# First value products ahead of the scores and of the last block's store, the next S5 unit's tables behind the key product, and one S5 scale from sums of squares

## The chip, the cores and the metric

One core of a Trainium2 chip runs the whole program: one layer of a sequence encoder for one sequence of 2048 positions. The metric is the device time of one launch in microseconds, as the median of several runs. A core has five engines, each with a queue of instructions that it takes strictly in order: TensorE (PE, matrix products and transposes), VectorE (DVE), ScalarE (ACT), GpSimd (POOL) and SyncE (SP, which here only issues DMAs). They wait for each other through semaphores.

## The reference, cut to what matters

```
h = rmsnorm(x, norm_mix_g);  p = h @ w_in
u, q_raw, k_raw, v, o_raw, i_raw, f_raw = split(p)      # 512 | 4x512 | 4 | 4
# S5: 32 groups of 16 channels, a diagonal complex state of 64 per group
x_t = a * x_{t-1} + B u_t;   y = Re(C x) + d * u
z = gelu(y);  z = z * sigmoid(z @ w_glu + b_glu);  y_ssm = rmsnorm(z)
# mLSTM: 4 heads of 128, gated matrix memory
q, k = silu(causal_conv4(q_raw, k_raw))
h = (decayed scores q k^T) v + q C_state, over its normaliser;  y_ml = rmsnorm(sigmoid(o) * h)
x = x + concat(y_ssm, y_ml) @ w_out
x = x + relu(rmsnorm(x) @ w_ff1)^2 @ w_ff2;  return rmsnorm(x)
```

## The kernel before

Every product that matters is made of float16 pairs: each operand is split into a high and a low half, and `mm3` issues three matmuls for each step over the 128 rows of the contraction (lines 168 to 170). So the weights are scaled by a power of two per matrix before they are split (`load_w`), and the S5 output `z` is scaled the same way before the GLU product.

The program has four stages. The start normalises x, transposes it into `xn`, and makes the S5 inputs and the gates. Then comes the mixer, which the change touches: one loop over 16 blocks `b`, block b being head b // 4 and quarter b % 4 of the positions (512 of them). Behind it stand the rest of the GLU with the output projection, and the feed-forward network, two thirds of the time, which the change leaves alone.

A turn of the mixer's loop issues, in the order of the text: `proj_qk(b+1, 0)`, the query product of the next block; `mix_store(b-1)`, which transposes the last block's output (`pT`, line 931), splits it (`mo`) and sends it to memory; `mix_scores(b)`, which makes the decay tables `sc` and `dm`, transposes the keys (`pK`, line 864) and multiplies keys by queries (`pS`, line 867); `proj_vo(b, 0)` and `proj_vo(b, 1)`, the value and output-gate products (`pv`), 48 matmuls each; between and behind them the S5 units; `mix_state(b)`; `proj_qk(b+1, 1)`, the key product; and `mix_out(b)`. `mix_out` ends with a chain that the store of the next turn needs: `og` on DVE (line 913), squares on ACT (915), a few 128x4 steps on DVE (918 to 920), a power on POOL (921), one more step on DVE (922), and the scaling of `og` on ACT (924). The transposes `pT` read that `og`. Behind the key or query product stand the convolution on DVE (three steps of line 256) and SiLU (lines 258 and 259).

The S5 part is cut into 16 units u of two groups. `s5_const(u)` makes the unit's tables: `inm` and `xt`, the small products `pgg` and `pit`, and the rotation table `rh` on POOL and DVE, which four DMAs on SP's queue copy into `rt` (line 696). `s5_state(u)` transposes the inputs (`put`), multiplies them (`pw`), rotates by `rt` on DVE and POOL (lines 722 to 724), scans (726), and rotates back into `sv`. `s5_out(u)` multiplies out (`py`, lines 744 and 745), makes the GELU (748 to 752: ACT squares, DVE, ACT tanh, DVE) and writes `uz`. After every fourth unit two reductions over 128x1024 elements (line 756) take the largest magnitude of `uz`, one for each half of the positions, into `zmx`; `glu_open` in block 11 makes a power of two for each half from it (lines 775 to 783).

The order in which the instructions stand on each engine is not that of the text. When the program is built, a list scheduler goes through it with durations of its own, takes for each engine the earliest instruction of the text that it believes to be ready, and fixes the queues. The text is its priority. So a changed order of calls moves instructions only as far as the scheduler follows, and the order it fixed does not change at run time. PSUM tiles are taken in turn from small pools: three banks tagged `ml` (`pT`, `pK`, `pS`, `pst`, `pn`, and the GLU's `pz` and `pgT`), three tagged `mm` (the large products), two tagged `ax` (the S5 products).

## Time and profile before

| | us |
|---|---|
| median of 3 runs (lowest to highest) | 2136.23 (2135.05 to 2136.75) |
| the profiled execution's own time | 2138.6 |
| its span, first to last instruction | 2136.9 |
| DVE busy in the stretch 140 to 563 us (most of the mixer) | 337.34 |
| ACT busy there | 236.25 |
| POOL busy there | 199.39 |

The profile is one execution. Its time is 2.4 us above the median, and 1.7 us of it lie outside the span. A row of the timeline gives the start, the duration, the engine, the line, and in brackets how long the engine had been idle before it and what ended that. Line numbers are those of the kernel before. Matmuls are pipelined: what a matmul costs is the distance to the next start, not its duration. Tile names in the rows of the order carry their block or unit: `pT5` is the store of block 5, `og11` the output of head 1, quarter 1, which is block 5, `pv120` the first value product of head 1, quarter 2, which is block 6.

### The profile page before, as it was taken

Reading aid. Unit: us, or ns where it says so; the run is one execution under the profiler, and the core shown is the slowest. Engines: PE = TensorE matmul, PEld = TensorE weight load, DVE = VectorE, ACT = ScalarE, POOL = GpSimd, SP = SyncE. Lnnn points to the kernel's source line nnn. Section 1 sums busy time; section 2 is a strip of 40 time slices with the busy share of each in tenths; the row PEclk is TensorE's granted clock in tenths of the full one; section 3 lists DMA queues with packets and bytes.
Section 4 is the critical chain, followed back from the end, with each engine's and each line's share of the span. In section 5 each row is a group of like instructions: output and inputs, shape, how many; then the busy total and the mean of one; then the engine's idle time right before and its main releaser. Section 6 shows DMA issues by size and latency. Waiting matters only on the chain.

```text
span 2136.9 us, 29966 instructions
## 1 busy us (share of the span) xinstructions
PE 2032.5 (95%) x11237; PEld 1157.3 (54%) x11237; DVE 1676.3 (78%) x2743; ACT 1080.7 (51%) x2027; POOL 1072.1 (50%) x976
## 2 busy tenths in 40 slices
PE   6999898998999999999999999999999999999997
PEld 4897676766667454444444444444444444444445
DVE  7887878886857776767888989987878787777775
ACT  4435556564545423365545545455655545555543
POOL 1014546453211102586766675585776666565644
PEclk9999999999999999999999999999999999999998
DMA  5111211111203242312122132124433322121012
GB/s 188 62 53 50 61 40 48 62 45 55 80 21 109 99 197 93 110 60 79 64 90 83 60 99 79 65 90 181 148 129 104 109 104 79 43 77 59 21 40 79
DMA packets 57027, 177.10 MB, mean 83 GB/s; under 512 B 8048, under 2 KB 21552, under 8 KB 43312
## 3 DMA queue, kind: packets, MB, share of 16 engines
q1 hardware_dynamic: 56880, 175.17, 24.5%
q8 instruction: 88, 1.44, 0.3%
q14 instruction: 59, 0.48, 0.1%
HBM read 138.35 MB, written 28.41 MB: 78 GB/s over the span
## 4 chain that ended last, share of the span: by engine, by line
PE 58%; DVE 22%; POOL 7%; issue 4%; DMA 4%; ACT 3%; SPq 1%; POOLq 0%; DVEq 0%; ACTq 0%
PE fx L1421 4%; PE fx L1422 4%; PE fx L1423 3%; PE gx L1421 3%; PE gx L1423 3%; PE gx L1422 3%; PE po L168 3%; PE po L169 3%; PE po L170 3%; DVE w2o L1288 3%; DVE y L256 2%; PE fv L1423 2%; PE fv L1422 2%; PE fv L1421 2%; DVE x L1517 2%
## 5 line engine op out<-in xcount | busy, mean ns | idle before, releaser
L1422 PEld LDWEIGHTS <-w2o 128*128 128x128 f16 x952 | 93.4, 98 | 123.8 <-issue 27.6
L1450 ACT ACTIVATE e<-e 128x512 f32<-128x512 f32 x96 | 60.3, 628 | 193.2 <-DVE e L1486 92.5
L1423 PEld LDWEIGHTS <-w2o 128*128 128x128 f16 x952 | 93.4, 98 | 105.0 <-DVE w2o L1288 3.6
L1421 PEld LDWEIGHTS <-w2o 128*128 128x128 f16 x952 | 93.7, 98 | 104.0 <-issue 2.7
L169 PE MATMUL pv<-w_vo,xn 128*128 128x256 f16 x512 | 142.2, 278 | 1.5 <-DVE w_vo L153 1.5
L168 PE MATMUL pv<-w_vo,xn 128*128 128x256 f16 x512 | 142.5, 278 | 0.8 <-ACT w_vo L152 0.7
L170 PE MATMUL pv<-w_vo,xn 128*128 128x256 f16 x512 | 142.4, 278 | 0.0
L1287 ACT ACTIVATE w2o<-r,fs_b 128x512 f16<-128x512 f32 (+1 forms) x96 | 78.9, 823 | 109.5 <-POOL r L1345 50.1
L1288 DVE SCALAR_TENSOR_TENSOR w2o<-r,fs_b,w2o 128x512 f16<-128x512 f32 (+1 forms) x96 | 104.5, 1091 | 25.7 <-ACT w2o L1287 25.4
L1517 DVE SCALAR_TENSOR_TENSOR x2b<-gx,dd,x2b 128x512 f32<-128x512 f32 x112 | 82.9, 745 | 43.4 <-PE gx L1423 43.1
L1345 POOL TENSOR_TENSOR r<-r,s 128x256 f32<-128x256 f32 x64 | 64.8, 1013 | 104.1 <-DVE w2o L1288 104.1
L1517 DVE SCALAR_TENSOR_TENSOR x<-gx,dd,x 128x512 f32<-128x512 f32 x128 | 94.4, 742 | 10.6 <-PE gx L1423 10.3
L168 PE MATMUL pq<-xn,w_qk 128*128 128x512 f16 x256 | 97.9, 383 | 0.0
L169 PE MATMUL pq<-xn,w_qk 128*128 128x512 f16 x256 | 97.5, 381 | 0.0
L1421 PE MATMUL fx<-hop,wB 128*128 128x512 f16 x256 | 97.1, 379 | 0.4 <-ACT e L1479 0.4
L170 PE MATMUL pq<-xn,w_qk 128*128 128x512 f16 x256 | 97.3, 380 | 0.0
L1422 PE MATMUL fx<-hop,wB 128*128 128x512 f16 x256 | 97.1, 379 | 0.0
L1423 PE MATMUL fx<-hop,wB 128*128 128x512 f16 x256 | 97.1, 379 | 0.0
L168 PEld LDWEIGHTS <-xn 128*128 128x128 f16 x768 | 88.3, 115 | 12.8 <-ACT xn L457 3.3
L170 PEld LDWEIGHTS <-xn 128*128 128x128 f16 x768 | 88.1, 115 | 10.6 <-issue 2.1
L169 PEld LDWEIGHTS <-xn 128*128 128x128 f16 x768 | 88.4, 115 | 9.2
L1301 POOL TENSOR_TENSOR s<-r 128x512 f32<-128x512 f32 x32 | 52.8, 1650 | 76.6 <-issue 65.8
(1378 smaller groups left out, 6911.0 us busy)
## 6 DMA issues: line engine op xcount, KB each, us to landing
r<-in_w_dram SPq DMA_DIRECT2D x64, 1024.0 KB, 4.9
xt<-in_xN_dram SPq DMA_DIRECT2D x16, 512.0 KB, 3.7
rt<-rh SPq DMA_DIRECT2D x64, 128.0 KB, 2.3
hopd<-ho SPq DMA_DIRECT2D x28, 256.0 KB, 2.6
hop<-hopd SPq DMA_DIRECT2D x7, 1024.0 KB, 4.9
st_vo<-in_wvo_dram SPq DMA_DIRECT2D x4, 1024.0 KB, 5.1
bcm<-negM_d SPq DMA_DIRECT2D x16, 256.0 KB, 3.2
ml_d<-mo SPq DMA_DIRECT2D x16, 256.0 KB, 2.4
```

The costliest lines, as they stand in the source:

```text
L168: T.matmul(out, wh, xh, start=(i == 0), stop=False)
L169: T.matmul(out, wh, xl, start=False, stop=False)
L170: T.matmul(out, wl, xh, start=False, stop=(i == n - 1))
L1287: S.activation(out=hi, in_=src, func=AF.Copy, scale=sg)
L1288: V.scalar_tensor_tensor(out=lo, in0=src, scalar=sg, in1=hi, op0=ALU.mult, op1=ALU.subtract)
L1301: G.tensor_tensor(out=s12[:, 0], in0=raw[:, 2], in1=raw[:, 3], op=ALU.add)
L1345: G.tensor_tensor(out=r[:, 1], in0=r[:, 1], in1=s12[:, 1], op=ALU.subtract)
L1421: T.matmul(out, wh, xh, start=(first and i == 0), stop=False, skip_group_check=True)
L1422: T.matmul(out, wh, xl, start=False, stop=False, skip_group_check=True)
L1423: T.matmul(out, wl, xh, start=False, stop=(last and i == n - 1), skip_group_check=True)
L1450: S.activation(out=x, in_=x if src is None else src, func=AF.Relu, scale=scale)
L1517: V.scalar_tensor_tensor(out=acc[:, j, c, :], in0=bk[b], scalar=dd, in1=acc[:, j, c, :], op0=ALU.mult, op1=ALU.add)
```

## The change

It has three parts. First, in each turn `proj_vo(b, 0)` and `mix_scores(b)` are issued ahead of `mix_store(b-1)`; in block 11 `proj_vo(11, 0)` so also stands ahead of the last S5 output and of `glu_open`. The last store, `mix_store(15)` behind the loop, stays where it was. Second, the tables of the next S5 unit are still issued right behind a unit's state where another unit of the same block follows, but behind the key product `proj_qk(b+1, 1)` where the unit is the block's last: that is ten of the fifteen units made inside the loop (2, 3, 5, 6, 8, 9, 11, 12, 14, 15). Third, the eight reductions of line 756 are gone; the ACT square of each unit also gives its sum over the free elements (`accum_out`), and `glu_open` makes one scale for both halves from the sixteen sums, by halving the exponent of their total.

```diff
+    def sq_pow2(ss, mp):
+        V.tensor_scalar(out=ss, in0=ss, scalar1=1e-30, scalar2=None, op0=ALU.max)
+        V.tensor_scalar(out=mp.bitcast(I32), in0=ss.bitcast(I32), scalar1=1, scalar2=None, op0=ALU.logical_shift_right)
+        V.tensor_scalar(out=mp.bitcast(I32), in0=mp.bitcast(I32), scalar1=0x7F800000, scalar2=None, op0=ALU.bitwise_and)
+        V.tensor_scalar(out=mp, in0=mp, scalar1=2.0 ** 64, scalar2=None, op0=ALU.mult)
...
-    zmx = gcon.tile([P, 2, 4], F32, name="zmx")
+    zss = gcon.tile([P, 16], F32, name="zss")
...
-        S.activation(out=y2, in_=py, func=AF.Square)
+        S.activation(out=y2, in_=py, func=AF.Square, accum_out=zss[:, u:u + 1])
...
-        if u % 4 == 3:
-            m = u // 4
-            for h in range(2):
-                V.tensor_reduce(out=zmx[:, h, m:m + 1], in_=uz[h][:, 8 * m:8 * m + 8, :].rearrange("p g n -> p (g n)"), axis=AX.X, op=ALU.max, apply_absolute_value=True)
...
-        zm, zi, zs, zd, zo = (gp.tile([P, 2], F32, name=f"z{n}") for n in "misdo")
-        V.tensor_reduce(out=zm, in_=zmx, axis=AX.X, op=ALU.max)
-        V.tensor_scalar(out=zm, in0=zm, scalar1=1e-6, scalar2=None, op0=ALU.max)
-        V.tensor_scalar(out=zi.bitcast(I32), in0=zm.bitcast(I32), scalar1=0x7F800000, scalar2=None, op0=ALU.bitwise_and)
+        zm, zi, zs, zd, zo = (gp.tile([P, 1], F32, name=f"z{n}") for n in "misdo")
+        V.tensor_reduce(out=zm, in_=zss, axis=AX.X, op=ALU.add)
+        sq_pow2(zm, zi)
...
         if b >= 1:
+            proj_vo(b, 0)
+        mix_scores(b)
+        if b >= 1:
             mix_store(b - 1)
-        mix_scores(b)
         if b == S5_BLOCKS:
...
-        if b >= 1:
-            proj_vo(b, 0)
...
             s5_state(u)
-            if u + 1 < 16:
+            if u + 1 < 16 and i + 1 < len(us_):
                 s5_const(u + 1)
...
         if 1 <= bn < 16:
             proj_qk(bn, 1)
+        if us_ and us_[-1] + 1 < 16:
+            s5_const(us_[-1] + 1)
```

How the queues moved is shown at three places. The first is block 10, on PE. Before, 33 of the 48 matmuls of `pv220` stand ahead of the store's transposes `pT9`, which are mixed with the key transposes and the scores, and the other 15 stand behind:

```order
L170 MATMUL pv220_6011<-w_vo2_4708,xn1_105 128x256
L931 MATMUL pT9_5970<-ident_72,og21_5634 128x128
L864 MATMUL pK10_5995<-ident_72,y221_5861 128x128 x2
...
L867 MATMUL pS10_5996<-y220_5582,y221_5861 128x128 x3
L168 LDWEIGHTS xn1_105
L168 MATMUL pv220_6011<-w_vo2_4708,xn1_105 128x256
```

After, on PE at the same place, all 48 matmuls, the key transposes and the scores stand ahead of `pT9`, and the S5 output `py14` comes right behind it:

```order
L177 MATMUL pv220_5967<-w_vo2_4704,xn1_105 128x256
L867 MATMUL pK10_6034<-ident_72,y221_5813 128x128 x4
L870 MATMUL pS10_6035<-y220_5576,y221_5813 128x128 x4
L934 MATMUL pT9_6047<-ident_72,og21_5590 128x128 x4
L751 MATMUL py14_6056<-m00_144,us14_5752 128x128
```

On ACT at that place, the scaling of `og21` (what `pT9` waits for) stood right behind the two halves of a weight split, and ahead of the evacuation of the key product `pq230`; before:

```order
L152 ACTIVATE w_qk3_5909<-st_qk3_5907,sg_qk3_5922 128x1024 x2
L924 ACTIVATE og21_5634<-og21_5634,v49_5897 128x128 x4
L245 ACTIVATE xc230_5960<-pq230_5934 128x512
L246 ACTIVATE y230_5959<-pq230_5934,cb2_4307,cw2_4305 128x512
L248 COPY xc231_6195<-hl221_5866 128x3
```

After, on ACT, that evacuation is ahead of it:

```order
L159 ACTIVATE w_qk3_5903<-st_qk3_5901,sg_qk3_5916 128x1024 x2
L252 ACTIVATE xc230_5954<-pq230_5928 128x512
L253 ACTIVATE y230_5953<-pq230_5928,cb2_4303,cw2_4301 128x512
L255 COPY xc231_6189<-hl221_5818 128x3
L927 ACTIVATE og21_5590<-og21_5590,v49_5891 128x128 x4
```

So `pT9` comes 15 matmuls, the key transposes and the scores later on PE, and `og21` three instructions later on ACT. In the other blocks the same table of rows, cut down to what stands ahead of `pT`, reads: in blocks 2 and 4, six matmuls of `pv` and `pK` and `pS` more than before; in blocks 3 and 7, `pK` and `pS` more and three matmuls less; in blocks 5 and 9, 23 matmuls and `pK` and `pS` more.

The second place is block 6, where the scheduler did otherwise. On PE before, the S5 output `py8` (eight rows, the last two shown) and two matmuls of the second value product stand ahead of `pT5`:

```order
L744 MATMUL py8_4437<-m00_144,us8_4133 128x128
L745 MATMUL py8_4437<-xt8_3809,sv8_4152 128x128
L168 LDWEIGHTS xn1_105
L168 MATMUL pv121_4452<-w_vo1_3083,xn1_105 128x256
L169 LDWEIGHTS xn1_105
L169 MATMUL pv121_4452<-w_vo1_3083,xn1_105 128x256
L931 MATMUL pT5_4345<-ident_72,og11_4007 128x128
L864 MATMUL pK6_4370<-ident_72,y121_4236 128x128 x2
```

After, on PE, `pK6` and `pS6` stand ahead of it and `py8` behind:

```order
L177 MATMUL pv120_4344<-w_vo1_3081,xn1_105 128x256
L867 MATMUL pK6_4411<-ident_72,y121_4190 128x128 x4
L870 MATMUL pS6_4412<-y120_3953,y121_4190 128x128 x4
L934 MATMUL pT5_4424<-ident_72,og11_3967 128x128 x4
L751 MATMUL py8_4433<-m00_144,us8_4129 128x128
```

On DVE, the small steps `v45` that lead to `og11` were mixed with the two halves of a weight split and a convolution step; before:

```order
L919 TENSOR_TENSOR v45_4272<-v45_4272,rc5_4250 128x4
L153 SCALAR_TENSOR_TENSOR w_qk2_4284<-st_qk2_4282,sg_qk2_4297,w_qk2_4284 128x1024
L920 TENSOR_SCALAR v45_4272<-v45_4272 128x4
L153 SCALAR_TENSOR_TENSOR w_qk2_4284<-st_qk2_4282,sg_qk2_4297,w_qk2_4284 128x1024
L256 SCALAR_TENSOR_TENSOR y130_4334<-xc130_4335,cw1_2051,y130_4334 128x512
L922 SCALAR_TENSOR_TENSOR v45_4272<-v45_4272,rc5_4250 128x4
```

After, on DVE, the step ahead of POOL's power comes first, and one half of the split lies between it and the last step:

```order
L922 TENSOR_TENSOR v45_4268<-v45_4268,rc5_4246 128x4
L923 TENSOR_SCALAR v45_4268<-v45_4268 128x4
L160 SCALAR_TENSOR_TENSOR w_qk2_4280<-st_qk2_4278,sg_qk2_4293,w_qk2_4280 128x1024
L925 SCALAR_TENSOR_TENSOR v45_4268<-v45_4268,rc5_4246 128x4
L160 SCALAR_TENSOR_TENSOR w_qk2_4280<-st_qk2_4278,sg_qk2_4293,w_qk2_4280 128x1024
```

So PE has not more but less work ahead of `pT5`, and DVE's steps for it come one half of a split sooner. The third place is ACT behind the loop, where the last store (whose call did not move) waits for `og33`; before:

```order
L811 ACTIVATE gth8_7993,vg8_7997<-zc8_7835 128x512
L144 ACTIVATE w_out2_8003<-st_o2_6416,sg_out2_8018 128x256 x8
L924 ACTIVATE og33_7775<-og33_7775,v415_7953 128x128 x4
L808 ACTIVATE gth9_8119<-gth9_8119 128x512
L827 ACTIVATE ms0_6361<-pgT7_8089 128x8x64
```

After, on ACT:

```order
L798 ACTIVATE zt9_7971<-pz9_7966 128x512
L151 ACTIVATE w_out2_7997<-st_o2_6464,sg_out2_8012 128x256 x4
L927 ACTIVATE og33_7733<-og33_7733,v415_7947 128x128 x4
L151 ACTIVATE w_out2_7997<-st_o2_6464,sg_out2_8012 128x256 x4
L811 ACTIVATE gth9_8113<-gth9_8113 128x512
```

Four of the eight pieces of the weight split moved behind `og33`. SP's queue keeps its order but for one pair: the store of block 10 now stands ahead of two loads in block 11 instead of behind them. On POOL the instructions of `rh` keep the order among themselves; of their neighbours one has changed sides with them, or with a step between them, in units 4, 7, 8, 10 and 15.

More of the change, by code (lines that the diff above doesn't have):

```diff
@@ L787, in glu_a @@
         gp = gl["p"]
-        zs = gl["z"][1][:, h:h + 1]
+        zs = gl["z"][1]
         zc = gp.tile([P, 512], F32, name=f"zc{n}", tag="zc", bufs=3)
@@ L801, in glu_b @@
         gp = gl["p"]
-        zi, _, zd, zo = (a[:, h:h + 1] for a in gl["z"])
+        zi, _, zd, zo = gl["z"]
         zc, zt = gl[n]
```

## The prediction

> **What bounds the kernel now.** I read the page first, then stretches of the span, then the waits of the mixer, then the chain of waits.
>
> ```profile
> span 2136.9 us, 29966 instructions
> 140.00:563.00 423.00, 390.21 (x2817) 303.24 (x2816) 337.34 (x663) 236.25 (x639) 199.39 (x207) 0.98 0.20 56
> 712.00:2000.00 1288.00, 1268.96 (x5907) 584.03 (x5906) 1024.73 (x1314) 643.57 (x957) 774.07 (x638) 1.00 0.27 92
> PE pT L931 <- ACT og L924: 20.3, 10, 3.9
> PE pgg L662 <- DVE t L722: 6.4, 4, 2.7
> ```
>
> In the two stretches the numbers behind the length are busy times of PE, weight loads, DVE, ACT and POOL, then the granted clock. In the feed-forward network PE is busy for 1268.96 of 1288 us, and nothing of the change is there. In the mixer it is busy for 390.21 of 423 us: 33 us are to be had. The last two rows are PE's waits of that stretch: ten times it waited at the store's transposes `pT` until ACT had scaled `og`, 20.3 us in all. That is what the first part of the change is about. These are the waits on which my sum rests, and two behind them (566.16 is the GLU's first product, 704.61 the last store):
>
> ```profile
> 227.49 0.33 PE L931 MATMUL pT<-ident,og 128*128 128x128 f32 x1 [1.61 <-ACT og L924]
> 263.81 0.62 PE L931 MATMUL pT<-ident,og 128*128 128x128 f32 x2 [2.34 <-ACT og L924]
> 373.72 0.33 PE L931 MATMUL pT<-ident,og 128*128 128x128 f32 x1 [3.91 <-ACT og L924]
> 514.96 0.47 PE L931 MATMUL pT<-ident,og 128*128 128x128 f32 x1 [3.25 <-ACT og L924]
> 566.16 0.61 PE L168 MATMUL pgl<-w_glu,zt 128*128 128x512 f16 x1 [2.13 <-ACT zt L795]
> 704.61 0.33 PE L931 MATMUL pT<-ident,og 128*128 128x128 f32 x1 [2.20 <-ACT og L924]
> ```
>
> Not every wait of PE is worth its length. The chain of waits runs through PE behind each of these six, but through the other ten-odd waits of the mixer it does not: there it runs on DVE, POOL and the copies of the rotation tables, and PE only follows. So I count a wait fully only where the chain passes it. Its share by line between 425 and 520 us shows how little PE it holds:
>
> ```profile
> by line: DVE y L256 13.6%; DMA rt<-rh 11.6%; issue 10.8%; SPq L696 7.5%; DVE t L726 6.1%; POOL rh L629 3.9%; POOL t L629 3.3%; DVE t L724 2.7%; POOL v L921 2.6%; DVE rh L632 2.4%; DVE t L722 2.1%; ACT w_qk L152 2.1%; DVE uz L752 2.1%; POOL
> ```
>
> **A wait costs more than its length.** Behind such a wait PE runs at half clock:
>
> ```profile
> 265.10:268.50 3.40, 3.40 (x19) 3.09 (x18) 3.40 (x6) 3.06 (x7) 1.33 (x2) 0.51 0.41 171
> 374.40:377.80 3.40, 3.40 (x18) 3.03 (x18) 3.07 (x5) 2.47 (x6) 1.06 (x3) 0.50 0.52 219
> 514.90:517.70 2.80, 2.74 (x13) 2.74 (x14) 2.42 (x3) 2.54 (x8) 0.00 (x0) 0.50 0.31 72
> 566.10:568.90 2.80, 2.74 (x7) 1.05 (x8) 2.77 (x5) 0.00 (x1) 0.00 (x0) 0.50 0.72 208
> 705.40:708.80 3.40, 3.17 (x14) 2.26 (x13) 3.32 (x10) 2.65 (x7) 0.00 (x0) 0.51 0.00 0
> ```
>
> The clock is the third number from the right. Each stretch is about 3.4 us long, so it holds 1.7 us of work less than at full clock. They follow waits of 2.34, 3.91, 3.25, 2.13 and 2.20 us; behind the 1.61 us at 227.49 there is none. A wait that shrinks below about 2 us should therefore also save 1.7 us.
>
> [...]
>
> **Part 1, the new order.** What is put ahead of `pT` is priced by the distance between starts:
>
> ```profile
> 196.32 0.38 PE L864 MATMUL pK<-ident,y 128*128 128x128 f32 x2
> 196.54 1.06 PE L867 MATMUL pS<-y,y 128*128 128x128 f32 x8
> 197.43 0.27 PE L169 MATMUL pv<-w_vo,xn 128*128 128x256 f16 x1
> 197.54 0.27 PE L170 MATMUL pv<-w_vo,xn 128*128 128x256 f16 x1
> 367.65 0.39 PE L744 MATMUL py<-m,us 128*128 128x128 f32 x2
> 369.44 0.27 PE L168 MATMUL pv<-w_vo,xn 128*128 128x256 f16 x1
> ```
>
> Two `pK` take 0.22 us, so four take 0.44; a block's scores take 0.89; a `pv` matmul 0.11; a whole `py` 369.44 - 367.65 = 1.79. `pK` and `pS` together are 1.33.
>
> Block 2: six `pv` and 1.33 make 1.99 us of work in a wait of 1.61: all of it goes, 1.6. Block 3: 1.33 less three `pv` is 1.0 of 2.34; 1.3 us remain, too short for the half clock: 1.0 + 1.7 = 2.7. Block 10: fifteen `pv` (1.65) and 1.33 make 3.0. But `og21` now stands behind three more instructions on ACT:
>
> ```profile
> 514.52 1.26 ACT L924 ACTIVATE og<-og,v 128x128 f32<-128x128 f32 x4
> 515.81 0.60 ACT L245 ACTIVATE xc<-pq 128x512 f32<-128x512 f32 x1
> 516.97 0.19 ACT L248 COPY xc<-hl 128x3 f32<-128x3 f32 x1
> ```
>
> From 515.81 to the end of the last one are 1.35 us by which `og21` comes later. The wait becomes 3.25 + 1.35 - 3.0 = 1.6; 1.65 + 1.7 = 3.3.
>
> Block 6 is the exception. `pT5` has 1.33 more ahead of it but loses `py8` and two `pv` (1.79 + 0.22), so PE comes to it 0.7 us sooner, and only an earlier `og11` helps. The chain that leads there:
>
> ```profile
> 354.89 1.13 DVE zmx L756
> 356.62 1.13 DVE zmx L756
> 369.63 1.20 DVE w_qk L153
> 370.83 0.09 DVE v L920
> 370.99 2.00 POOL v L921
> ```
>
> Two of the removed reductions lie on it (2.26 us; they are part 3, but paid here), and the half of the weight split ahead of line 920 (1.2) now stands behind it, beside POOL's power. That is 3.46 of the 3.91 us, and the slow stretch: 5.2. `py8` follows the wait instead of filling the time ahead of it, which costs nothing as long as the wait is gone.
>
> The last store: four pieces of the weight split no longer stand ahead of `og33`.
>
> ```profile
> 700.97 3.30 ACT L144 ACTIVATE w_out<-st_o,sg_out 128x256 f16<-128x256 f32 x8 [1.12 <-DVE sg_out L125]
> ```
>
> Half of 3.30 is 1.65 of the 2.20 us; with the slow stretch 3.3.
>
> The store's own work, its two splits and its DMA, only shifts. Nothing reads what it stores before the loop's end, and on SP it passes two loads in block 11 alone. Its bank of PSUM is next taken by `pn`, which stands a whole key product later, so nobody waits for it. In block 6 `pK6` may wait a moment for its key (line 259 on DVE); that step lies on the chain of `og11` and comes sooner with it, so it adds nothing behind.
>
> **Part 2, the tables.** Their work stays the same, DMAs included. It is moved past the key product on PE, past its convolution on DVE, and, on SP and POOL, past nothing: there the rows of `rh` keep their order. I cost it at nothing. What hides it is the time between the tables and the next unit's rotation. The trace shows no case with them later, so bounds: a gain of 6.4 us, if PE's waits at `pgg` (quoted above) all go, and a loss, worked out below as a rival. I take zero, since the order hardly follows the text here.
>
> **Part 3, the scale.** Eight reductions leave DVE. Two are counted in block 6, two stand between the GLU's weight load and its product:
>
> ```profile
> 555.39 0.68 DVE L869 TENSOR_TENSOR kw<-pK,gcol 128x512 f32<-128x512 f32 x1
> 556.65 2.34 DVE L756 TENSOR_REDUCE zmx<-uz 128x1 f32<-128x1024 f32 x2
> L915 ACT ACTIVATION_READ_ACCUMULATOR kw<-og x64: 185/187/218, 182.4 to 698.2; 128x1 f32 x64
> ```
>
> There 2.3 us go. `kw` moves ahead into the wait for the load, while a step of the same size (`y215`) comes in its place. Two more steps on 128x1 elements come in. The product waited 2.13 us; that wait goes, and its slow stretch: 2.1 + 1.7 = 3.8. The other four reductions are off the chain. Against it, sixteen sums are read out on ACT, 0.19 us each as in the last row (a square with the same read-out elsewhere), 3.0 us; ACT is on the chain only here and there, so I charge a third, 1.0.
>
> **The sum.** 1.6 + 2.7 + 3.3 + 5.2 + 3.3 + 3.8 - 1.0 = 18.9 us. I don't take all of it. Behind each wait the chain goes back to DVE and POOL for some 10 to 80 us, and there the queues were dealt out anew as well, in places for the worse (`og21` above). I take two thirds, 12.6, a choice and not a row. The profiled execution took 2138.6 us, so it would take 2126.0; the median of the runs is 2.4 below it. So the forecast is 2123.7 us.
>
> **The rivals.**
>
> *The waits go and come back elsewhere.* PE comes sooner to places that DVE, POOL or a table's copy sets, as in the shares above. Then only the two pairs of reductions and little else count, within 4 us: about 2134. For it speaks how little PE the chain holds from 425 to 520 us; against it that the six waits I count are those which the chain passes.
>
> *All waits at `pT` go, on the chain or not.* The ten waits, each cut by what the order puts ahead of it in blocks 1 to 10: 0.6, 1.6, 1.0, 2.0, 1.1, 3.5, 1.0, 1.0, 1.1, 1.6, which is 14.5 of the 20.3; 2.1 and 1.7 behind them; six slow stretches (a sixth follows the wait of block 4), 10.2; less 1.0. That is 27.5: 2138.6 - 27.5 - 2.4 = 2108.7. Against it: PE isn't on the chain there.
>
> *Only DVE's part acts*, the scheduler having kept PE's order where it mattered, as in block 6: 3.5 and 2.1 and no slow stretch, 5.6 less 1.0: 2131.6. The shown rows of block 10 speak against it.
>
> *The slow stretches stay.* They might hang on the pattern of work around, not on the wait alone. [...] The five rows speak against it. [...]
>
> *Slower: the tables come late.* The scheduler may let the three convolution steps go ahead of DVE's half of `rh`, and a late copy stops the rotation at once. The rows are the first and the last of the eight copies on the chain, a convolution step, and a rotation that waited:
>
> ```profile
> 195.20 2.32 DMA rt<-rh
> ...
> 496.66 2.36 DMA rt<-rh
> 372.01 0.75 DVE L256 SCALAR_TENSOR_TENSOR y<-xc,cw,y 128x512 f32<-128x512 f32 x1
> 481.62 0.69 DVE L722 TENSOR_TENSOR t<-pw,rt 128x512 f32<-128x512 f32 x1 [1.25 <-DMA rt<-rh]
> ```
>
> Three steps are 2.25 us for a unit, 22.5 for the ten that moved. The chain passes eight of fifteen copies, so 12.0 of it would show. PE would lose its gain to these waits, and only DVE's part (4.6 as above) would stay: 12.0 - 4.6 is 7.4 more than the median of 2136.2, 2143.6. The sign turns when four of the ten units come late (4 x 2.25 x 8/15 = 4.8). The last row shows that there is no slack; the kept order of `rh` on POOL speaks against it.
>
> **How the numbers follow.** The chances: forecast 0.47; waits come back 0.16; all go 0.12; slow stretches stay 0.10; only DVE's part 0.06; slower 0.09. The range takes in all but the last, with some room: 2108 to 2138. About 0.2% (4.3 us) is what a measurement of this kernel can tell from no change: faster 0.75, same 0.16, slower 0.09.
>
> **What would show it.** Right: the waits that stood at 263, 373, 514 and 704 us are below 2 us, no half clock stands behind them, PE's waits on `og` from 140 to 563 us sum to less than 8 us, and the GLU's first product doesn't wait. Wrong: the same idle time of PE in the mixer under other names, `pgg`, `py` or `put`; rows of line 722 waiting for `rt` by 2 us or more; or a wait at `pT5` as long as before, since there the order gives PE nothing to do.

## The result and the profile after

The changed kernel takes 2120.91 us (median of 4 runs, 2116.55 to 2122.24), the kernel before 2135.64 us (4 runs, 2131.21 to 2136.75): a ratio of 0.9926, with a 95% interval of 0.9911 to 0.9941. The forecast was 2123.7 us. Measured once more on another chip (`e9_again`, below), the gain was 13.9 us instead of 14.7.

The page, the stretches and the waits of PE in the mixer, for the changed kernel, in the columns that the prediction used. Line numbers are now those of the changed kernel: `pT` is line 934, the scaling of `og` 927, `pgg` 669, the rotation's first step 729.

```profile
span 2118.6 us, 29982 instructions
```

```profile
140.00:553.00 413.00, 386.93 (x2801) 299.65 (x2798) 331.85 (x657) 239.04 (x660) 199.26 (x207) 0.99 0.20 57
712.00:2000.00 1288.00, 1269.47 (x5919) 584.40 (x5918) 1025.79 (x1311) 645.82 (x956) 778.45 (x640) 1.00 0.27 92
```

```profile
PE pgg L669 <- DVE t L729: 9.9, 5, 3.2
PE pT L934 <- ACT og L927: 6.7, 6, 1.5
PE py L752 <- POOL sv L741: 3.3, 6, 0.9
PE pgg L669 <- DVE uz L759: 2.4, 2, 1.2
```

The same piece of the mixer is 10 us shorter. The waits at `pT` fell from 20.3 to 6.7 us, those at `pgg` grew from 7.0 (6.4 + 0.6) to 12.3, and those at `py` from 2.1 to 4.3. PE's idle time as a whole fell only from 32.8 us (423.00 - 390.21) to 26.1 (413.00 - 386.93): half of what went at `pT` came back elsewhere. The rows of the timeline at the places of the prediction (blocks 3, 6, 10 and the last store), and two waits that are new or longer, at `pgg3` and at `pst`:

```profile
261.95 0.33 PE L934 MATMUL pT<-ident,og 128*128 128x128 f32 x1 [1.34 <-ACT og L927]
367.81 0.33 PE L934 MATMUL pT<-ident,og 128*128 128x128 f32 x1 [1.32 <-ACT og L927]
507.69 0.62 PE L934 MATMUL pT<-ident,og 128*128 128x128 f32 x2
687.96 0.33 PE L934 MATMUL pT<-ident,og 128*128 128x128 f32 x1 [0.81 <-ACT og L927]
219.88 0.40 PE L669 MATMUL pgg<-xt,ge 128*128 128x16 f32 x2 [3.17 <-DVE t L729]
555.36 0.80 PE L889 MATMUL pst<-vt,kw 128*128 128x129 f32 x2 [2.28 <-DVE C L894]
```

Between the first scores and the feed-forward network PE ran at half clock in eight windows of 3.4 us before and in three after. The third of these stands at the opening of the GLU, where one stood before (at 565.5 us); the other two are new. The clock is the third number from the right:

```profile
220.40:223.90 3.50, 3.50 (x19) 2.81 (x19) 3.46 (x9) 1.31 (x3) 1.29 (x1) 0.51 0.02 5
476.40:479.90 3.50, 3.50 (x19) 2.52 (x18) 3.46 (x7) 0.87 (x2) 1.66 (x2) 0.51 0.00 0
555.00:558.40 3.40, 3.04 (x8) 1.41 (x9) 3.17 (x8) 0.00 (x0) 0.00 (x0) 0.51 0.65 205
```

Where the time went can be read from the first matmul of some tiles on PE in the two timelines (us from the start of the span). Each line's gain is the step of the shift from the line above it; beside it the term of the prediction's sum, before the two thirds. The last column tells how many matmuls more (or less) than before PE runs between the two marks: where it isn't 0, the new order has moved matmuls across a mark, and gain or loss is in part only that.

| PE's first matmul of | before | after | shift | gained | term | matmuls |
|---|---|---|---|---|---|---|
| `pS0`, the first scores | 164.73 | 161.89 | -2.84 | | not of the change | |
| `pw2`, in block 1 | 211.46 | 209.30 | -2.16 | -0.7 | | 0 |
| `pw3`, block 2 | 242.20 | 240.34 | -1.86 | -0.3 | 1.6 | 0 |
| `pw5`, block 3 | 283.94 | 279.50 | -4.44 | 2.6 | 2.7 | -10 |
| `pw8`, blocks 4 and 5 | 348.67 | 346.93 | -1.74 | -2.7 | | +13 |
| `pw9`, block 6 | 387.46 | 381.08 | -6.38 | 4.6 | 5.2 | -3 |
| `pw14`, blocks 7 to 9 | 494.47 | 488.03 | -6.44 | 0.1 | | +3 |
| `pw15`, block 10 | 531.96 | 520.96 | -11.00 | 4.6 | 3.3 | -3 |
| `pgl3`, the GLU's opening | 599.52 | 588.93 | -10.59 | -0.4 | 3.8 | 0 |
| `po0`, with the last store | 706.49 | 691.43 | -15.05 | 4.5 | 3.3 | +4 |
| `fx`, feed-forward network | 902.75 | 886.79 | -15.96 | 0.9 | | -4 |
| end of the span | 2136.86 | 2118.64 | -18.22 | 2.3 | not of the change | |

So only sums of lines with equal work can be held against the terms. Idle is the time in which PE ran no matmul:

| stretch | gained | terms | idle before, after | windows at half clock |
|---|---|---|---|---|
| block 1 | -0.7 | | 2.1, 2.8 | 0, 0 |
| block 2 | -0.3 | 1.6 | 4.3, 3.2 | 0, 1 |
| blocks 3 to 6 | 4.5 | 7.9 | 11.3, 10.4 | 3, 0 |
| blocks 7 to 10 | 4.6 | 3.3 | 13.4, 8.1 | 1, 1 |
| the GLU's opening | -0.4 | 3.8 | 3.9, 3.9 | 1, 1 |
| last store, up to `fx` | 5.4 | 3.3 | 7.9, 6.7 | 3, 0 |

From the first scores to the network, where the change acts, 13.1 us are gained. The 2.8 and 2.3 us outside are the spread of single executions: the profiles of `e2_tables` and `e3_scale`, below, which gain nothing, are 3.9 and 1.6 us earlier than that of before at the first scores too.

### The profile page after: what moved, and what is told of

It reads as the page before. It is cut to its first block, busy times and chain, and to the rows that moved or that the text cites. A ratio compares the mean times of both kernels' runs of the same rounds, so it can differ in the third digit from the quotient of the medians.

```text
span 2118.6 us, 29982 instructions
## 1 busy us (share of the span) xinstructions
PE 2024.7 (96%) x11237; PEld 1152.8 (54%) x11237; DVE 1670.2 (79%) x2737; ACT 1080.5 (51%) x2043; POOL 1074.6 (51%) x976
## 4 chain that ended last, share of the span: by engine, by line
PE 56%; DVE 25%; DMA 6%; POOL 6%; issue 4%; ACT 3%; SPq 1%; POOLq 0%; DVEq 0%; ACTq 0%
PE fx L1426 3%; PE fx L1428 3%; PE fx L1427 3%; PE gx L1428 3%; PE gx L1426 3%; PE gx L1427 3%; DMA r<-in_w_dram 3%; DVE w2o L1293 3%; PE po L177 3%; PE po L176 3%; PE po L175 3%; DVE x L1522 2%; DVE y L263 2%; PE fv L1428 2%; PE fv L1427 2%
```

## The experiments

All of them in one table. The last three columns are counted from each run's trace, between the first scores and the first `fx`: length, time in which PE ran no matmul, and windows at half clock. They belong to one execution each, the times and ratios to all. Each ratio is against the kernel before on the same chip.

| run | parts | us (runs) | ratio, 95% | length | idle | half clock |
|---|---|---|---|---|---|---|
| before | | 2135.64 (4) | | 738.0 | 42.8 | 8 |
| changed | 1, 2, 3 | 2120.91 (4) | 0.9926, 0.9911 to 0.9941 | 724.9 | 35.0 | 3 |
| `e1_order` | 1 | 2123.48 (5) | 0.9941, 0.9926 to 0.9956 | 728.3 | 36.0 | 4 |
| `e2_tables` | 2 | 2134.31 (12) | 0.9992, 0.9981 to 1.0004 | 738.0 | 43.3 | 7 |
| `e3_scale` | 3 | 2135.41 (12) | 0.9996, 0.9983 to 1.0010 | 735.4 | 42.0 | 6 |
| `e4_order_scale` | 1, 3 | 2125.13 (6) | 0.9945, 0.9928 to 0.9962 | 727.0 | 30.3 | 8 |
| `e5_values_first` | half of 1 | 2130.78 (10) | 0.9970, 0.9957 to 0.9983 | 734.3 | 36.9 | 9 |
| `e6_scores_first` | half of 1 | 2124.04 (4) | 0.9944, 0.9926 to 0.9963 | 726.2 | 37.4 | 2 |
| `e7_split_later` | all, and more | 2125.92 (6) | 0.9949, 0.9931 to 0.9966 | 726.9 | 34.7 | 6 |
| `e8_scale_split_later` | 3, and more | 2140.18 (1) | | 741.2 | 42.0 | 12 |
| `e9_again` | 1, 2, 3 | 2122.90 (6) | 0.9944, 0.9924 to 0.9964 | 725.3 | 32.4 | 5 |
| `e10_tables_held` | all, and more | 2126.71 (12) | 0.9960, 0.9946 to 0.9975 | 728.1 | 32.9 | 7 |
| `e11_order_tables` | 1, 2 | 2127.81 (12) | 0.9961, 0.9945 to 0.9976 | 728.5 | 35.9 | 4 |
| `e12_tables_in_gap` | all, and more | 2119.85 (6) | 0.9930, 0.9910 to 0.9949 | 722.1 | 30.5 | 4 |

### The parts one by one

`e1_order` makes only part 1 of the change:

```diff
         if b >= 1:
+            proj_vo(b, 0)
+        mix_scores(b)
+        if b >= 1:
             mix_store(b - 1)
-        mix_scores(b)
...
-        if b >= 1:
-            proj_vo(b, 0)
```

> Part 1 alone on the kernel before: first value products ahead of the scores, the store of the last block's output behind them; tables and scale as before. Theory A (the order of PE's work carries the change): by the prediction's terms without the two pairs of reductions (2.3 and 2.1 us) and without the read-outs (+1.0), 18.9 - 4.4 + 1.0 = 15.5, two thirds 10.3: 0.9952 of the time before (0.994 to 0.997), and the waits of PE at pT of blocks 3, 6 and 10 and of the last store below 2 us. Theory B (the eight reductions carry it, the order is cover that the chain does not need): above 0.998, with the wait at pT5 still above 3 us. Theory C (every new deal of the queues shifts the time by some us in either direction, the parts do not add up): anything from 0.995 to 1.003 and no sum of parts.

0.9941: a little more gain than Theory A's number, within its range. Part 1 alone gives most of the gain, and Theory B is refuted. The last store's wait went to 0.81 us; of the waits named only that at `pT5` stayed above 2:

```profile
372.07 0.33 PE L931 MATMUL pT<-ident,og 128*128 128x128 f32 x1 [2.27 <-ACT og L924]
```

`e2_tables` makes only part 2:

```diff
-            if u + 1 < 16:
+            if u + 1 < 16 and i + 1 < len(us_):
                 s5_const(u + 1)
...
+        if us_ and us_[-1] + 1 < 16:
+            s5_const(us_[-1] + 1)
```

> Part 2 alone on the kernel before: the next unit's tables issued behind the key product. The prediction costs it at nothing: 0.999 to 1.001, with PE's waits at pgg as before (6 to 7 us in all). Theory B agrees. Its rivals: 0.997 if the waits at pgg go (6.4 us), 1.005 if the copies of the rotation tables come late (line 722 then waits for rt by 2 us or more in some units). Theory C: any of 0.997 to 1.003.

0.9992, and the mixer's waits at `pgg` and `pT` are those of before (6.9 and 20.4 us): nothing, as costed.

`e3_scale` makes only part 3 (the reductions go, the sums of squares come):

```diff
-        S.activation(out=y2, in_=py, func=AF.Square)
+        S.activation(out=y2, in_=py, func=AF.Square, accum_out=zss[:, u:u + 1])
...
-                V.tensor_reduce(out=zmx[:, h, m:m + 1], in_=uz[h][:, 8 * m:8 * m + 8, :].rearrange("p g n -> p (g n)"), axis=AX.X, op=ALU.max, apply_absolute_value=True)
```

> Part 3 alone on the kernel before: the scale of the gated unit's input from sums of squares, eight reductions gone, sixteen read-outs on ACT. Theory A: 2.3 us at pT5, 2.1 at the first product of the gated unit, and its slow stretch 1.7 (that of block 6 stays, since 1.6 us or more of the wait remain), less 1.0 for the read-outs: 5.1, two thirds 3.4: 0.9984 (0.997 to 1.000), with the wait at pT5 between 1 and 2 us. Theory B: 0.995 or less, almost all of the change's gain. Theory C: 0.996 to 1.003.

0.9996: the time agrees with Theory A's upper end, but the wait at `pT5` does not. It grew to 4.78 us. The timeline shows why for ACT, the engine that scales `og11`, and for PE:

```profile
367.12 2.19 ACT L159 ACTIVATE w_qk<-st_qk,sg_qk 128x1024 f16<-128x1024 f32 x2 [2.43 <-DVE sg_qk L134]
369.33 0.60 ACT L252 ACTIVATE xc<-pq 128x512 f32<-128x512 f32 x1
369.82 0.77 ACT L253 ACTIVATE y<-pq,cb,cw 128x512 f32<-128x512 f32 x1
370.48 0.19 ACT L255 COPY xc<-hl 128x3 f32<-128x3 f32 x1
370.57 1.28 ACT L927 ACTIVATE og<-og,v 128x128 f32<-128x128 f32 x4
```

```profile
371.03 0.47 PE L934 MATMUL pT<-ident,og 128*128 128x128 f32 x1 [4.78 <-ACT og L927]
```

`og11` is scaled 2.7 us sooner than before (370.57 against 373.27), but 2.2 us of that had been there since unit 8's `pw8`. Within block 6 the reductions brought about half a microsecond, since ACT now does both halves of a weight split and a convolution's first steps right ahead of `og11`. The row of before had shown that ACT was close behind DVE there:

```profile
373.27 1.28 ACT L924 ACTIVATE og<-og,v 128x128 f32<-128x128 f32 x4 [1.94 <-DVE v L922]
```

ACT's own queue had been done only 1.94 us ahead of it. In `e3_scale` the split also starts 1.5 us later, counted from `pw8`, since it waits for a step on DVE (`sg_qk`). PE comes sooner too, and waits longer.

`e4_order_scale` makes parts 1 and 3, both shown.

> Parts 1 and 3 together, the tables as before. Since part 2 is costed at nothing, Theories A and B: the time of the changed kernel, 0.9926 of the time before (0.991 to 0.9945), with PE's waits at pgg near 12 us as in the changed kernel. If part 2 carries a share, this comes out above 0.9945. Theory C: differs from the changed kernel by 3 us or more in either direction, although the order of instructions is almost the same.

0.9945, within the range and just at its end; the waits at `pgg` are 10.4 us instead of 12.3. With almost the changed kernel's order it has less idle time on PE (30.3 against 35.0 us) and eight windows at half clock instead of three; its profile is the slowest of its six runs. It is 4.2 us slower than the changed kernel, the sign that Theory C named; but the changed kernel itself, measured again, gave 0.9944, so this is not a difference of the two kernels. The last section returns to it.

### What of part 1 does it

`e5_values_first` puts the first value products ahead of the store and leaves the scores behind it; `e6_scores_first` does the reverse.

```diff
+        if b >= 1:
+            proj_vo(b, 0)
         if b >= 1:
             mix_store(b - 1)
         mix_scores(b)
...
-        if b >= 1:
-            proj_vo(b, 0)
```

```diff
+        mix_scores(b)
         if b >= 1:
             mix_store(b - 1)
-        mix_scores(b)
```

> Half of part 1: the first value products ahead of the store and of the scores, the store still ahead of the scores. Counted from the order and the durations of the prediction, PE then has 0.7 us more work ahead of pT in blocks 2 and 4, 2.5 in blocks 5 and 9, 1.9 in block 10, 2 to 3.5 in the gated unit's blocks 13 to 15, nothing in blocks 3, 7, 8 and 11, and 1.1 less in block 6. Theory A (a wait is worth the work that is put ahead of it): of the mixer's waits 0.6 + 0.7 + 1.2 + 1.1 + 1.9 go, with one slow stretch 1.7 it is 7.2, two thirds 4.8: 0.9977 (0.9965 to 0.9990), the waits of block 3 (2.3), 6 (3.9) and 8 (2.3) as before. Rival D (the value products are the whole of part 1): 0.9945 or less. Rival E (only the scores ahead of the store count): above 0.9995.

> The other half of part 1: the scores ahead of the store, the first value products behind it as before. Counted in the same way, PE has 0.3 to 0.5 us more ahead of pT in blocks 1, 2, 3, 7 and 11, 0.9 in blocks 5 and 9, 1.3 in block 10, 0.6 less in block 8, nothing in blocks 4 and 6, 2.6 less in block 12. Theory A: 0.5 + 0.5 + 0.35 + 0.9 + 0.35 + 0.9 + 1.3 = 4.8, one slow stretch 1.7, two thirds 4.3, less what block 12 gives back: 0.998 (0.997 to 0.9995). Rival D: above 0.9995. Rival E: 0.9945 or less. If neither half comes below 0.997, part 1 works only whole.

`e5_values_first` came out at 0.9970, as worked out by Theory A. `e6_scores_first` came out at 0.9944, as good as the whole of part 1 and outside Theory A's range. So no theory held for both: the count of work put ahead of `pT` missed the scores, and Rival E, right for the scores, is refuted by what the value products alone gain. The halves don't add up. Rows of the timeline of `e6_scores_first` on PE:

```profile
367.36 0.30 PE L864 MATMUL pK<-ident,y 128*128 128x128 f32 x1 [3.78 <-DVE v L920]
508.96 0.30 PE L864 MATMUL pK<-ident,y 128*128 128x128 f32 x1 [2.28 <-DVE v L918]
689.84 0.33 PE L931 MATMUL pT<-ident,og 128*128 128x128 f32 x1 [0.81 <-ACT og L924]
```

In blocks 6 and 10 the wait is still there, only at `pK` now, and PE's idle time as a whole fell by 5.4 us (42.8 to 37.4). The rest of the 11.8 us, 6.4, is time in which the same matmuls ran faster: two windows are at half clock instead of eight. And the last store, for which no order of the loop should matter, gained: 0.81 us of wait as in `e1_order`, against 2.20 in `e5_values_first`. The scheduler had dealt ACT's queue there anew with the scores' place: in `e6_scores_first` four of the eight pieces of the weight split stand behind `og33`, in `e5_values_first`, as before, all eight ahead of it. What the scores' place does inside the mixer and what this deal does behind it was not taken apart.

### What held block 6

`e7_split_later` and `e8_scale_split_later` take ACT's weight split away from `og11`: the load stays, the split comes a block later.

```diff
         if b % 4 == 1 and 4 < b < 13:
-            load_qk(b // 4 + 1)
+            st_k = stg.tile([P, KD, 256], F32, name=f"st_k{b}", tag="stg")
+            nc.sync.dma_start(out=st_k, in_=wqk[b // 4 + 1])
...
             mix_store(b - 1)
+        if b in (6, 10):
+            load_qk(b // 4 + 1, st_k)
```

> The changed kernel with one more edit: the query-key weights of the next head are loaded where they were, but split into halves one block later, behind the store (blocks 7 and 11 instead of 6 and 10). In block 6 of the changed kernel ACT does this split (2.19 us) and the first steps of a convolution right ahead of the scaling of og11, and PE waits 1.32 us at pT5. If that split is what took the place of the reductions and of DVE's half as the last thing ahead of og11, the wait at pT5 goes below 0.4 us; the time gains 1.3 us: 0.992 (0.990 to 0.9935). Rival: og11 is then held by POOL's power and DVE's steps ahead of it, the wait stays above 0.9 us and nothing is gained. Second rival: the split comes late for the next key product or pushes og12 back; then a wait of 2 us or more appears in block 7 or at pq20: 0.994 or more.

> Part 3 alone (as in e3_scale) with that same later split of the query-key weights. In e3_scale the two reductions of block 6 had left DVE, yet PE's wait at pT5 was 4.78 us, with ACT's split of 2.19 us and a convolution's first steps right ahead of og11. If that split swallowed the gain, the wait at pT5 falls by about 2 us, to 2.3 to 3.0, or og11 is scaled that much sooner. If the gain was lost elsewhere (POOL's power, or the reductions were no part of the path), the wait stays above 4 us. One look: the wait decides, not the time.

The rows of `e7_split_later` on PE:

```profile
368.29 1.20 PE L934 MATMUL pT<-ident,og 128*128 128x128 f32 x4 [0.29 <-ACT og L927]
408.61 0.28 PE L669 MATMUL pgg<-xt,ge 128*128 128x16 f32 x1 [2.81 <-DVE t L729]
442.48 0.33 PE L934 MATMUL pT<-ident,og 128*128 128x128 f32 x1 [3.30 <-ACT og L927]
```

At `pT5` 0.29 us are left: the split was what held `og11`. But two waits came in its place, 2.81 us at a `pgg` and 3.30 at a later `pT`, and the time is 2125.92: no gain, as the second rival had it. In `e8_scale_split_later`, a single run, the wait grew to 5.54 us, but `og11` is scaled 1.7 us sooner than in `e3_scale` (368.89 against 370.57), and what holds it now is POOL's power with the step behind it (line 925):

```profile
368.89 1.28 ACT L927 ACTIVATE og<-og,v 128x128 f32<-128x128 f32 x4 [2.87 <-DVE v L925]
```

```profile
369.34 0.48 PE L934 MATMUL pT<-ident,og 128*128 128x128 f32 x1 [5.54 <-ACT og L927]
```

The expectation's two signs so came out on different sides: the wait is above 4 us, but the scaling is sooner by most of the 2 us that were expected. So in block 6 three things stand close behind each other ahead of `og11`: DVE's steps with the reductions (the scaling starts at 373.27 us), ACT's split (370.57), POOL's power (368.89). Taking one away pays up to the next.

### What held block 2

The wait at `pgg3`, of 3.17 us, ate block 2's term. Before, it was this:

```profile
221.57 0.40 PE L662 MATMUL pgg<-xt,ge 128*128 128x16 f32 x2 [2.70 <-DVE t L722]
```

A `pgg` needs a bank of PSUM that the rotation's first step (line 722, after the change 729) frees. The timeline of the changed kernel on DVE ahead of that step:

```profile
214.42 0.46 DVE L618 TENSOR_TENSOR bt<-bcA,ssi 128x128 f32<-128x128 f32 x1 [0.26 <-DMA bcA<-in_s5bc_dram]
214.80 1.35 DVE L618 TENSOR_TENSOR bt<-bcA,sim 128x128 f32<-128x128 f32 x1
216.07 1.28 DVE L626 TENSOR_SCALAR bcA<-bcA,sgn 128x128 f32<-128x128 f32 x1
...
218.74 0.28 DVE L625 TENSOR_TENSOR bcA<-bcA,bt 128x128 f32<-128x128 f32 x1
218.95 0.28 DVE L624 TENSOR_TENSOR bcA<-bcA,bt 128x128 f32<-128x128 f32 x1
219.15 0.68 DVE L729 TENSOR_TENSOR t<-pw,rt 128x512 f32<-128x512 f32 x1
```

Seven steps on `bcA`, a table for units 8 to 11, stand ahead of unit 2's rotation; the scheduler put them there. Unit 8 needs them at its `pgg`, at 333.7 us. `e10_tables_held` holds this table back until unit 4 and the next until unit 8; `e12_tables_in_gap` holds only this one, until unit 2 (with `if v == 2` and element 2). `e9_again` is the changed kernel itself, `e11_order_tables` parts 1 and 2.

```diff
+        if v >= 2:
+            S.copy(bcA[:, 0, 0, 0:1], zss[:, (0, 0, 4, 8)[v]:(0, 0, 4, 8)[v] + 1])
         nc.sync.dma_start(out=bcA, in_=s5bc[:, :, 8 * v:8 * v + 8, :])
```

> The changed kernel once more, to stand on the same chip beside the next two: 0.9911 to 0.9941 as in its first runs. The stretches at half clock should not stand where they stood in its first profile if they hang on how a wait falls into a fixed grid of 3.41 us; if they hang on the waits alone, they follow the same three waits (3.17, 1.52 and 2.28 us) again.

> The changed kernel with one edit: the tables of units 8 to 11 and 12 to 15 (bcA) are held back until unit 4 and unit 8 are done, by one copy of an element ahead of their load. In the kernel before and the changed one the seven steps of the first of these tables stand in DVE's row right ahead of unit 2's rotation, the first reader that frees pgg3's bank, and wait for their load: 214.2 to 219.2 us in the changed kernel, where PE waits 3.17 us at pgg3. If that swallowed block 2's 1.6 us of the prediction, the wait at pgg3 goes below 1 us and block 2 is 2 to 4 us shorter; the seven steps (about 3 us of DVE) come back in blocks 4 and 7, where a wait may grow: 0.9915 of the time before, 0.990 to 0.993, at best better than the changed kernel by 0.15%. Rival: the wait at pgg3 has another cause (unit 3's own tables or POOL), stays above 2 us, and the time is that of the changed kernel.

> Parts 1 and 2 together, the scale as before (eight reductions on DVE, no read-outs). If part 3 is worth what its terms in the prediction say (2.3 in block 6, 2.1 and perhaps 1.7 at the gated unit, less 1.0, two thirds of it), this is 3 us slower than the changed kernel: 0.994. If, as e1_order against e4_order_scale suggests, part 3 adds nothing that can be measured once the order is changed, it is 0.992 to 0.9935. If part 2 works only with part 3, it equals e1_order, 0.994, with PE's waits in the same places.

In `e10_tables_held` the wait at `pgg3` is gone; in block 4, where the seven steps stand now (287 to 294 us), there is a longer one:

```profile
215.06 0.29 PE L671 MATMUL pgg<-xt,ge 128*128 128x16 f32 x2
```

```profile
300.44 0.33 PE L936 MATMUL pT<-ident,og 128*128 128x128 f32 x1 [4.16 <-ACT og L929]
```

The cause was right, the expected gain was not there: 0.9960, outside the range of 0.990 to 0.993. In the changed kernel DVE waits 3.36 us for PE a little later in block 2, and there the last run put the seven steps:

```profile
240.54 0.35 DVE L894 SCALAR_TENSOR_TENSOR C<-C,gbc,pst 128x129 f32<-128x129 f32 x1 [3.36 <-PE pst L889]
```

> The changed kernel with the tables of units 8 to 11 alone held back, until unit 2 instead of unit 4: in DVE's row their seven steps now stand ahead of line 894, where DVE waits 3.36 us for PE at 240.5 us in the changed kernel. In e10_tables_held the wait at pgg3 went (3.25 us to none), but the steps then fell into block 4, where PE waited 4.16 us at pT3. If the gain of block 2 is real and only the place of those steps was bad, the wait at pgg3 is gone here too, no wait at pT3 comes in its place, and the way from the first scores to the feed-forward network is 2 to 4 us shorter than the changed kernel's 725: 0.9925 of the time before (0.991 to 0.9945), faster than the changed kernel by 0.1%. Rival: PE, freed in block 2, waits the same 2 to 3 us at the next place that DVE or a rotation table's copy sets (pT2, pgg5, pgg6, py4), and the 725 us stay.

Its rows on PE and on DVE:

```profile
218.73 0.29 PE L671 MATMUL pgg<-xt,ge 128*128 128x16 f32 x2
...
228.53 0.38 PE L754 MATMUL py<-xt,sv 128*128 128x128 f32 x1 [1.42 <-POOL sv L743]
```

```profile
217.46 0.68 DVE L731 TENSOR_TENSOR t<-pw,rt 128x512 f32<-128x512 f32 x1
...
238.65 0.29 DVE L620 TENSOR_TENSOR bt<-bcA,ssi 128x128 f32<-128x128 f32 x1 [1.45 <-DMA bcA<-in_s5bc_dram]
238.86 0.28 DVE L620 TENSOR_TENSOR bt<-bcA,sim 128x128 f32<-128x128 f32 x1
239.06 0.28 DVE L628 TENSOR_SCALAR bcA<-bcA,sgn 128x128 f32<-128x128 f32 x1
```

No wait at `pgg3`, none at `pT3` above 0.6 us, and 722.1 us from the first scores to the network against 724.9 and 725.3: 2.8 and 3.2 us less, as worked out; 2.0 of them lie in block 2, between `pw2` and `pw3` (29.1 us against 31.05 and 31.1). The time, 2119.85 us, is the lowest of all, but its interval holds both of the changed kernel's ratios, so it can't be called faster than the changed kernel.

`e9_again` gave 0.9944 and `e11_order_tables` 0.9961, 4.9 us more, which is the side expected if part 3 counts, but the intervals overlap. And `e4_order_scale` against `e1_order` says that it does not count (0.9945 and 0.9941). The wait at `pT5` tells more: 2.27 and 2.32 us in `e1_order` and `e11_order_tables`, which keep the reductions, 1.32, 0.90 and 0.19 us in the changed kernel, `e9_again` and `e4_order_scale`, which drop them. So part 3 shortens that wait by one or two us once the order is changed; whether the whole kernel gains by it stays open within about 0.2%. The same holds for part 2 behind the new order: without part 3 the time goes from 0.9941 to 0.9961 with it, with part 3 from 0.9945 to 0.9926 or 0.9944.

## Why the prediction was right, and where it was not

**The number.** The terms sum to 18.9 us, of which two thirds were taken; 13.1 were gained where the change acts. That the fraction came out is luck. By the table of stretches three places fell short by 9.5 us (block 2 by 1.9, blocks 3 to 6 by 3.4, the GLU by 4.2), block 1 lost 0.7, two places gave 3.4 more than their terms, and the 1.0 us charged for the read-outs has no place of its own. The direction and the size are right because part 1 carries the change, as said (`e1_order`); the sum by places is not.

**Blocks 3 to 6: 4.5 us for 7.9.** The two waits did what was worked out: 1.34 us are left at `pT2` where 1.3 was said, 1.32 at `pT5`. The half clock behind both is gone, and a third window with it. But PE's idle time there fell by 0.9 us only, although the waits at `pT` fell from 10.0 to 3.3: between 265 and 341 us new ones stand at `pgg`, `py` and `pit` (1.2, 1.8, 0.9, 1.6, 0.5 and 1.0). That is the rival "the waits come back elsewhere", and its sign, idle time under the names `pgg` and `py`, is met in part. No run was made for these places. The traces only tell that the wait of 1.5 us at `pgg8` stands in `e1_order` and `e5_values_first`, which put the value products first, and is 0.45 in `e6_scores_first`, which doesn't.

**Blocks 7 to 10: 4.6 us for 3.3.** The wait in block 10, to be 1.6 us, vanished. The sum for it was right in what it had, but ACT's split ahead of `og21` began 2.9 us behind the first matmul of `pv220` instead of 4.5, and that was in no term: luck. The waits at `pT6` to `pT8`, counted as nothing since the chain does not pass them, fell by 2.5 us. The half clock of block 10 went, and another came at 476 us.

**The last store: 5.4 us for 3.3.** Its wait fell to 0.81 us, and besides the half clock at 705 us that at 688 (two windows) went, which no term had.

**Block 2: -0.3 us for 1.6** ("all of it goes"). The wait at `pT1` went, but `pgg3`, ahead of it, waits 3.17 instead of 2.70 us and is followed by half clock. The prediction had quoted that wait as part 2's and not asked what stood before it; it was a table on DVE, as `e10_tables_held` and `e12_tables_in_gap` show.

**The GLU: -0.4 us for 3.8.** The product waits no more, but `pst`, two matmuls ahead, waits 2.28 us for line 894 on DVE, and the half clock stayed too. The rows of DVE and SP in the changed kernel show what the term left out:

```profile
550.80 0.43 DVE L775 TENSOR_SCALAR bg<-bg 128x512 f32<-128x512 f32 x1 [2.51 <-DMA bg<-in_bglu_dram]
552.58 2.47 DVE L160 SCALAR_TENSOR_TENSOR w_glu<-st_glu,sg_glu,w_glu 128x1024 f16<-128x1024 f32 x2
554.97 0.34 DVE L894 SCALAR_TENSOR_TENSOR C<-C,gbc,pst 128x129 f32<-128x129 f32 x1
```

```profile
534.66 0.33 SPq L140 DMA_DIRECT2D st_glu<-in_wglu_dram  x1
545.77 0.32 SPq L940 DMA_DIRECT2D ml_d<-mo  x1
546.23 0.34 SPq L774 DMA_DIRECT2D bg<-in_bglu_dram  x1
```

The 2.3 us of the two reductions turned into a wait of DVE for `bg`, the GLU's bias. That load is one of the two which the store of block 10 now passes on SP ("on SP it passes two loads in block 11 alone", priced at nothing). In the seven profiles with SP's old order (before, `e2_tables`, `e3_scale` and `e5_values_first` to `e8_scale_split_later`) `bg` is issued 0.5 us behind `st_glu`, the load of the GLU's weights, and DVE doesn't wait for it; here it stands 11.6 us behind, right after the store. In the seven with the new order DVE waits for it: 1.4 to 2.5 us in the five without the reductions, 0.1 and 0.6 in the two that keep them (`e11_order_tables`, `e1_order`). What an earlier load would bring is open: `e7_split_later` has one, and `pst` waits 2.75 us all the same, since there the split of `w_glu`, which stands ahead of line 894 in both, waits for ACT.

**Part 2** costed at nothing: `e2_tables` agrees, 0.9992.

**Part 3** was credited with 2.3 us in block 6 "on the chain". Alone it gave half a microsecond there, as ACT's split stood right behind (`e3_scale`, `e8_scale_split_later`); with part 1, one to two. The chain of waits names what ended last, not how close the second was.

**Part 1** carried the change, as said, but not quite as said. Its work ahead of `pT` was priced by matmuls; `e6_scores_first` gets all of the gain with less of them. Of the 9.7 us that `e1_order` is shorter between the first scores and `fx`, 6.8 are idle time and 2.9 faster matmuls.

**The slow stretches** were priced too high, at 1.7 us each. In the 14 profiles PE runs the same 4448 matmuls between the first scores and `fx`; the time in which it runs them goes from 688.7 us with two windows at half clock (`e6_scores_first`) to 699.2 with twelve (`e8_scale_split_later`), about 1.0 us for each by a straight line through all 14.

**The rivals.** "Only DVE's part acts" and "tables late" are refuted by `e1_order` and `e2_tables`. "All waits at `pT` go" is refuted too: 6.7 us of them are left, and the time is 12 us above its number. "The waits come back" is true in part, as above. "Slow stretches stay": four of the five named went and the GLU's stayed; which waits bring one is not as the prediction had it (below). Of the other signs, the waits on `og` were to sum to less than 8 us and came to 6.7, and behind the four waits at `pT` no half clock stands in this profile.

## What to carry to other kernels

A wait on one engine is worth what lies between it and the second-latest thing that could have ended it; look for that second one (the queue of the engine that releases, row by row) before the wait is counted. Work moved out of a wait pays only where the next engine has a gap: in single profiles the same seven steps gave 3 us in a gap of DVE and cost as much two blocks later. A transfer that a new order puts ahead of another on its queue can delay that other until its own data are there (here the load of `bg` was issued 11.6 us behind `st_glu` instead of 0.5); ask who reads it. Compare stretches only between marks with the same work in between. Count the time at half clock beside the idle time: of the 13.1 us here 7.8 were idle time and 5.3 faster matmuls.

## What the runs showed of the hardware

**When the clock halves.** The prediction took it that a wait above about 2 us halves the clock for 3.4 us. In 14 profiles every half-clock stretch starts on a grid of 3.413 us of its execution (in the kernel before, the starts at 265.13, 299.27 and 374.36 us are 10 and 22 windows apart), and what goes ahead of it is idle time of PE within one such window. Counted over all full-clock windows of the 14 profiles from 140 to 2000 us:

| PE idle in a window | windows | half clock in the next |
|---|---|---|
| below 1.3 us | 7286 | 0 |
| 1.3 to 1.9 us | 144 | 25 |
| 1.9 to 2.1 us | 26 | 19 |
| above 2.1 us | 52 | 52 |

So in these profiles above 2.1 us, 0.62 of a window, half clock always followed (52 of 52), below 1.3 us, 0.38 of one, never (0 of 7286); in between (44 of 170) the idle time alone didn't decide. A wait of 2 to 3 us so halved the clock or not by how it fell on the grid, which lay elsewhere in each execution (a start at 220.45 us in the changed kernel, at 219.8 in `e9_again`): before, the 2.70 us at `pgg3` were cut into windows with 1.89 and 0.80 us of idle time, and no half clock followed. In `e9_again` the three stretches of the changed kernel came back (at 219.8, 475.8 and 554.3 us), which by its expectation speaks for the waits alone; but two more came, at 335.8 and 690.8. The first of them stands behind the wait at `pgg8`, 1.56 us in the changed kernel and 1.55 here: there the two windows that it touches hold 0.94 and 1.10 us of idle time, here 0.61 and 1.41. So here the place on the grid made the difference. This can be why `e4_order_scale` has eight windows with nearly the same order, and it fits the spread of one kernel's runs: the 23 runs of before beside `e9_again` go from 2130.59 us at a granted clock of 0.988 to 2143.42 us at 0.980, with a correlation of -0.95 between time and clock.

**DVE beside POOL.** The steps on `bcA` of 128x128 elements take 0.28 us in `e12_tables_in_gap`, and 1.35 and 1.28 us in the changed kernel at 214.80 and 216.07. They end at 216.15 and 217.35, just behind two instructions of POOL:

```profile
214.69 1.31 POOL L863 TENSOR_TENSOR sc<-sc,y 128x512 f32<-128x512 f32 x1
215.97 1.31 POOL L730 TENSOR_TENSOR t<-t,rt 128x512 f32<-128x512 f32 x1
```

These end at 216.00 and 217.28; in `e12_tables_in_gap` POOL is idle while the seven steps run. The 14 profiles have 392 such steps on `bcA` and its products `bt`. The 219 with no POOL instruction beside them take 0.25 to 0.29 us. Of the others, 110 take 0.31 to 1.40 us, and each of these ends 0.08 to 0.15 us behind the end of a POOL instruction; 63 run beside one and still take 0.27 to 0.30. So 110 of the 173 short DVE steps that met a POOL instruction lasted until one of POOL's had ended, and where the scheduler put such a step changed its price by more than four times (0.28 us against 1.35 and 1.28).
